# When a pair of weight blocks is asked for, and what stands in line behind its mixing: first pass of a decoder layer on one core

## The chip, the core and the metric

The kernel runs on one core of one Trainium2 chip. The metric is the device time of one execution in microseconds (us). The engines are TensorE (PE, with PEld for its weight loads), VectorE (DVE), ScalarE (ACT) and GpSimd (POOL); each works through its own queue strictly in order. SyncE (SP) issues all DMA transfers here, also in order: an entry that waits holds up every entry behind it.

## The reference

One layer over a sequence of 1024 positions and 2048 channels: x is projected by `w_in`, eight attention heads with a forget gate, a short convolution and a pooling branch work on the projections, each branch is gated, and everything is projected back and normalised:

```python
proj = einsum('bsd,de->bse', x, w_in)
q, k, v, g_att, fg, c_b, c_c, c_h, g_conv, p_u, g_pool = split(proj)
y = concat([attention(q, k, v, fg) * silu(g_att),
            short_conv(c_b, c_c, c_h) * silu(g_conv),
            pool(p_u) * silu(g_pool)])
out = layer_norm(alpha * x + einsum('bse,ed->bsd', y, w_out))
```

All is float32. A matmul operand is split into a rounded part and a remainder, and three matmuls stand for one.

## The kernel before, in words

Both projections are computed by a Strassen-Winograd scheme: the operands are cut in 2 x 2 blocks and seven block products take the place of eight. The weight columns of the input projection come as 28 pairs (`Pair`, N_PAIRS); a pair has four raw blocks of 128 x 1024 (512 KB each), numbered 0 to 3. From them are mixed T1 = block 1 - block 0, T2 = block 3 - T1, T3 = block 3 - block 1 and T4 = block 2 - T2 (`mix`, `mix_last`; T1 and T2 on DVE, T3 and T4 on POOL). T4 is stored to memory (`store_mixed`, t_dram) for the second pass.

The first pass (`first_pass`, up to the end of the pool "first") computes four products of every pair: "11" with block 0, "s2" with T2, "s1" with T1 and "s3" with T3. A product is 8 x 3 matmuls of 512 columns (`multiply`). For the pairs 0 to 11 (AHEAD) the product "11" is done at the start. The pairs are then worked in the order 0, 12, 1, 13, ..., 11, 23, 24 to 27; the index in this order is the place n. So an even place up to 22 has three products (s2, s1, s3) and an odd place four (11, s2, s1, s3).

While a product runs, the operand of the next one is split: ACT casts the rounded part (L121, "hi"), DVE subtracts it (L122, "lo"); both need two of four buffers h1, which come free when the product before has ended. The third matmul of a product is the first that needs lo. `beside(p, name)` says what else is issued after each product: the mixing of the pair at place n+1, the loading of the pair at place n+2 (`load_place`), the eight blocks s4 of x (`make_s4`, four loads of 256 KB from xt, three subtractions on DVE, one store to s4_dram), and the mixing of the output weights (`OutBlocks`: four loads from w_out, four subtractions on POOL, four stores to o_dram).

The order on each queue is set by a scheduler that runs when the program is built: it takes an instruction as soon as its model of the engines finds its inputs and a buffer ready, so it may pull an instruction in front of others that stand before it in the code. `tc.keep_in_program_order` pins an instruction to its place in the code. Raw blocks and T3 share nine buffers w1; s4 and the output weights use four buffers wr and some of wh. A load into a buffer waits for the last reader of what was in it. Each transfer also waits until the eighth before it has landed, since there are eight completion semaphores.

Of the kernel before, what the change touches and what calls it, by code (L numbers as in the profile page):

```python
# [36 lines left out]
ALU = mybir.AluOpType  # L37
# [4 lines left out]
S = 1024  # L42
# [3 lines left out]
H = S // 2  # L46
# [5 lines left out]
KH = KT // 2  # L52
N_PAIRS = 28
WARM_UP = 8
EARLY = 8
AHEAD = 12
# [17 lines left out]
def layer(ctx: ExitStack, tc: tile.TileContext, xt, x, wp, wf, b_f, conv_w, pool_w, pool_scale,  # L74
          w_out, ln_g, ln_b, out):
    nc = tc.nc
# [27 lines left out]
    def f4(name, tag):  # L104
        return tile_of([P, S], F32, name, tag)
# [50 lines left out]
    t_dram = dr.tile([N_PAIRS, P, S], F32, tag="td", name="t_dram")  # L156
    s4_dram = dr.tile([KH, P, H], F32, tag="s4d", name="s4_dram")
    sy_dram = dr.tile([4, KH, P, H], F32, tag="syd", name="sy_dram")
    o_dram = dr.tile([2, 4, KH, P, H], F32, tag="od", name="o_dram")
# [81 lines left out]
    class Pair:  # L241
# [12 lines left out]

        def mix(self):
            r = self.raw
            self.t3 = f4("t3", "w1")
            nc.gpsimd.tensor_tensor(self.t3, r[3], r[1], ALU.subtract)  # L258
            nc.vector.tensor_tensor(r[1], r[1], r[0], ALU.subtract)  # L259
            nc.vector.tensor_tensor(r[3], r[3], r[1], ALU.subtract)  # L260

        def mix_last(self):
            r = self.raw
            nc.gpsimd.tensor_tensor(r[2], r[2], r[3], ALU.subtract)  # L264

        def store_mixed(self):
            nc.sync.dma_start(t_dram[self.p], self.raw[2])

        def early(self, acc):

# [4 lines left out]
        def products(self):  # L275

            def start():
                self.ca = f4("ca", "c")
                if self.p < AHEAD:
                    nc.sync.dma_start(self.ca[:, :H], a_dram[self.p, :, :H])  # L280

            def p6():
                if self.ca is None:
                    start()
                self.b = bank("aux")
                return self.b

            def after_p6():
                self.u2 = half("u2", "wh")
                nc.vector.tensor_tensor(self.u2, self.b, self.ca[:, :H], ALU.add)  # L290

            def p5():
                self.c = bank("acc")
                return self.c

            def after_p5():
                self.cb = f4("cb", "c")
                nc.vector.tensor_tensor(self.cb[:, :H], self.c, self.u2, ALU.add)

            def after_p7():  # L300
                nc.vector.tensor_tensor(self.ca[:, H:], self.b, self.ca[:, :H], ALU.add)
                nc.vector.tensor_tensor(self.cb[:, H:], self.c, self.ca[:, H:], ALU.add)
                nc.sync.dma_start(a_dram[self.p], self.ca)
                nc.sync.dma_start(b_dram[self.p], self.cb)

            yield self, lambda: self.raw[3], "s2", p6, after_p6
            yield self, lambda: self.raw[1], "s1", p5, after_p5
            yield self, lambda: self.t3, "s3", lambda: self.b, after_p7

        def first_product(self):  # L310
# [46 lines left out]
            nc.tensor.transpose(turned[:, st], flat[:, st * P : st * P + P], ident[: 2 * NH, : 2 * NH])  # L357
        return turned

    def make_s4(k):  # L360
        r21, r22, r11, r12 = (half("xr", "wr") for _ in range(4))
        for r, e, h in ((r21, k, 1), (r22, KH + k, 1), (r11, k, 0), (r12, KH + k, 0)):
            nc.sync.dma_start(r, xt[e, :, h * H : h * H + H])
        nc.vector.tensor_tensor(r21, r21, r22, ALU.add)
        nc.vector.tensor_tensor(r21, r21, r11, ALU.subtract)
        nc.vector.tensor_tensor(r12, r12, r21, ALU.subtract)
        nc.sync.dma_start(s4_dram[k], r12)

    class OutBlocks:
# [5 lines left out]
        def load(self):  # L375
            i, k = self.i, self.k
            self.t = [half("wo", tag) for tag in ("wr", "wr", "wr", "wh")]
            for t, e, c in zip(self.t, (KH + k, KH + k, k, k), (0, 1, 0, 1)):
                nc.sync.dma_start(t, w_out[e, :, i * S + c * H : i * S + c * H + H])

        def mix(self):
            b11, b12, b21, b22 = self.t
# [6 lines left out]

        def store(self):  # L390
            for j, t in enumerate(self.t):
                nc.sync.dma_start(o_dram[self.i, j, self.k], t)

    pairs = [Pair(p) for p in range(N_PAIRS)]
    banks = [bank("acc") for _ in range(4)] + [bank("aux") for _ in range(4)]
# [54 lines left out]
    def load_place(n):  # L450
        order[n].load(0, 1, 3, 2)

    def beside(p, name):
# [10 lines left out]
        n = place[p]  # L464
# [3 lines left out]
        if name == "s2" and n < N_PAIRS - 2:  # L468
            pairs[p].store_mixed()
            if n - 1 in outs:  # L470
                outs[n - 1].store()
            if n in outs:
                outs[n].load()
        if name == "s1":
            if n in outs:
                outs[n].mix()
            if n in gate_sums_at:
                env["sums"] = gate_sums(gate_sums_at[n], 0)
        if name == "s3":
            if n + 2 < N_PAIRS:  # L480
                load_place(n + 2)
            if 3 <= n < 7:
                make_s4(2 * n - 6)
                make_s4(2 * n - 5)
            if n == 2:
                nc.vector.tensor_copy(fgt[:, :4], turned_sums(env["sums"]))
            if n == 3:
                nc.vector.tensor_tensor(fgt[:, 4:], fgt[:, :4], turned_sums(env["sums"]), ALU.subtract)
# [6 lines left out]
        if (n, name) == (N_PAIRS - 1, "s1"):  # L495
            replace("s4", "xc", s4_dram)
            for q in (0, 1):
                t = half("c11", "wr")
# [8 lines left out]

    banks_set = deque()
    env, gate_sums_at = {}, {2: "11", 3: "s3"}
    outs = {7 + n: OutBlocks(n % 2, n // 2) for n in range(2 * KH)}  # L510

    def first_pass():
        ahead_of = in_order()
# [739 lines left out]
```

## Time and profile before

| | us |
|---|---|
| median of 3 runs | 1677.95 (1676.4 to 1681.62) |
| profiled execution | 1684.7 |
| span of its trace | 1682.9 |

The start (products "11" of the first pairs) takes the first 85 us, the rest of the first pass lasts to about 692 us; then come the second pass with the attention, and the output projection. The output weights are mixed at the places 7 to 22, which lie between about 230 us and 575 us. PE is the busiest engine (1572.4 us); TensorE's granted clock is 0.973 of full speed on average. In the tables a wait is put down to what ended last, "x" is a count of instructions, and a time in a window counts from the start of the span.

### The profile page before, as it was taken

How to read it: one execution, taken by the hardware profiler on the slowest of the kernel's cores; microseconds unless marked ns; L12 is line 12 of the kernel's file. 1: busy time of each engine (PE TensorE's matmuls, PEld its weight loads, DVE VectorE, ACT ScalarE, POOL GpSimd, SP SyncE). 2: the span in 40 equal slices, each digit the busy share in tenths (PEclk: the TensorE clock that was granted, in tenths of full speed). 3: DMA queues.
4: the chain of work that ended last, by engine and by line, in shares of the span. 5: the costliest groups of instructions: out<-in, count | busy, mean ns of one | idle time of the engine just before them, and what ended most of it. 6: DMA issues, size and time to landing. Idle time of an engine off the chain costs nothing. (4 is left out here: it accounts for less than half of the span.)

```text
span 1682.9 us, 20233 instructions
## 1 busy us (share of the span) xinstructions
PE 1572.4 (93%) x6836; PEld 1268.7 (75%) x6836; DVE 1101.1 (65%) x1587; ACT 701.6 (42%) x1254; POOL 511.1 (30%) x381
## 2 busy tenths in 40 slices
PE   7999999899889899999999999989988899999985
PEld 6777887777767788788878787867766777788765
DVE  6786445445555445468777777776779875567777
ACT  4412221111111124457575757656665554434431
POOL 0133245555556521002222222342426221100005
PEclk9999999999999999999999999999999999999998
DMA  8986567778777754735454545445445446557562
GB/s 240 337 294 231 203 213 271 269 269 280 259 268 252 266 210 153 272 111 183 155 182 158 174 168 165 154 137 183 141 143 168 149 140 216 185 179 232 181 190 100
DMA packets 156808, 339.93 MB, mean 202 GB/s; under 512 B 17952, under 2 KB 27040, under 8 KB 156704
## 3 DMA queue, kind: packets, MB, share of 16 engines
q1 hardware_dynamic: 156704, 338.64, 59.7%
q8 instruction: 53, 0.87, 0.2%
q14 instruction: 51, 0.42, 0.1%
HBM read 247.28 MB, written 91.29 MB: 201 GB/s over the span
## 5 line engine op out<-in xcount | busy, mean ns | idle before, releaser
L122 DVE TENSOR_TENSOR wh<-wr,wh 128x512 fp32r<-128x512 f32 x272 | 204.8, 759 | 93.7 <-ACT wh L121 93.3
L121 ACT CAST wop<-wb 128x1024 fp32r<-128x1024 f32 x76 | 79.9, 1052 | 329.0 <-PE acc L129 199.7
L121 ACT CAST wh<-wr 128x512 fp32r<-128x512 f32 x272 | 166.5, 618 | 92.9 <-PE acc L130 34.4
L130 PE MATMUL aux<-xs,wop 128*128 128x512 f32 x448 | 178.7, 399 | 18.4 <-DVE wop L122 18.4
L128 PE MATMUL acc<-x,wh 128*128 128x512 f32 x448 | 178.7, 399 | 3.9 <-ACT wh L121 3.9
L130 PE MATMUL acc<-x,wh 128*128 128x512 f32 x448 | 177.7, 397 | 1.9 <-DVE wh L122 1.9
L128 PE MATMUL aux<-xs,wop 128*128 128x512 f32 x448 | 177.3, 396 | 0.0
L129 PE MATMUL aux<-xs,wop 128*128 128x512 f32 x448 | 177.2, 395 | 0.0
L129 PE MATMUL acc<-x,wh 128*128 128x512 f32 x448 | 176.1, 393 | 0.0
L122 DVE TENSOR_TENSOR wop<-wb,wop 128x1024 fp32r<-128x1024 f32 x76 | 126.1, 1659 | 55.0 <-ACT wop L121 55.0
L258 POOL TENSOR_TENSOR t<-wb,wb 128x1024 f32<-128x1024 f32 x28 | 69.7, 2490 | 304.0 <-DMA wb<-wp 131.2
L130 PEld LDWEIGHTS aux<-xs,wop 128*128 128x128 f32 x448 | 86.0, 192 | 39.7 <-DVE wop L122 21.6
L259 DVE TENSOR_TENSOR wb<-wb,wb 128x1024 f32<-128x1024 f32 x28 | 37.5, 1340 | 119.3 <-POOL t L258 119.3
L130 PEld LDWEIGHTS acc<-x,wh 128*128 128x128 f32 x448 | 84.6, 189 | 27.1 <-DVE wh L122 9.2
L128 PEld LDWEIGHTS acc<-x,wh 128*128 128x128 f32 x448 | 84.8, 189 | 23.7 <-ACT wh L121 8.2
L128 PEld LDWEIGHTS aux<-xs,wop 128*128 128x128 f32 x448 | 86.1, 192 | 18.1
L129 PEld LDWEIGHTS aux<-xs,wop 128*128 128x128 f32 x448 | 85.7, 191 | 18.3
L129 PEld LDWEIGHTS acc<-x,wh 128*128 128x128 f32 x448 | 84.9, 190 | 15.6
L264 POOL TENSOR_TENSOR wb<-wb,wb 128x1024 f32<-128x1024 f32 x28 | 81.7, 2919 | 38.9 <-DVE wb L260 36.0
L130 PE MATMUL acc<-xs,wh 128*128 128x512 f32 x224 | 88.1, 393 | 3.0 <-DVE wh L122 2.9
L688 POOL TENSOR_TENSOR m<-m,t 128x256 f32<-128x256 f32 (+1 forms) x64 | 69.9, 1092 | 62.7 <-ACT t L741 59.0
L121 ACT CAST wop<-t 128x1024 fp32r<-128x1024 f32 x28 | 29.5, 1054 | 141.3 <-PE aux L129 83.2
(265 smaller groups left out, 3859.8 us busy)
## 6 DMA issues: line engine op xcount, KB each, us to landing
wb<-wp SPq DMA_DIRECT2D x116, 512.0 KB, 5.7
wr<-wp SPq DMA_DIRECT2D x112, 256.0 KB, 2.9
wo<-w_out SPq DMA_DIRECT2D x64, 256.0 KB, 5.2
o_dram<-wo SPq DMA_DIRECT2D x64, 256.0 KB, 3.0
wr<-o_dram SPq DMA_DIRECT2D x64, 256.0 KB, 2.8
t_dram<-wb SPq DMA_DIRECT2D x28, 512.0 KB, 3.8
a_dram<-ca SPq DMA_DIRECT2D x28, 512.0 KB, 6.0
b_dram<-cb SPq DMA_DIRECT2D x28, 512.0 KB, 6.1
```

Source lines behind the costliest of these rows:

```text
L121: nc.scalar.copy(hi, src)
L122: nc.vector.tensor_tensor(lo, src, hi.bitcast(F32), ALU.subtract)
L128: nc.tensor.matmul(acc, wh, xh, start=start, stop=False, **more)
L129: nc.tensor.matmul(acc, wh, xl, start=False, stop=False, **more)
L130: nc.tensor.matmul(acc, wl, xh, start=False, stop=stop, **more)
L258: nc.gpsimd.tensor_tensor(self.t3, r[3], r[1], ALU.subtract)
L259: nc.vector.tensor_tensor(r[1], r[1], r[0], ALU.subtract)
L264: nc.gpsimd.tensor_tensor(r[2], r[2], r[3], ALU.subtract)
L688: eng.tensor_tensor(kept[n][:, c0:], prev[:, c0:], t[n, j][:, c0:], op)
```

## The change

Four things change in the first pass. (1) `load_place(n + 2)` is issued after product s1 of place n, where it was after s3. (2) For the pairs 0 to 11, whose block 0 is no longer needed, T1 is written over block 0, T2 into a new buffer and T3 over block 1; the instructions stand in the order T1, T2, T3. For the other pairs all stays as it was: T3 into a new buffer first, then T1 over block 1 and T2 over block 3. (3) The loads and stores of the output weights, the store of T4 and the loads of s4 are pinned to their place in the code; the s4 blocks are loaded after one product and mixed after the next of s2 and s3, from place 3 to place 7. (4) The output weights are mixed at the places 7 to 24 without 14 and 18.

```diff
         def mix(self):
             r = self.raw
-            self.t3 = f4("t3", "w1")
-            nc.gpsimd.tensor_tensor(self.t3, r[3], r[1], ALU.subtract)
-            nc.vector.tensor_tensor(r[1], r[1], r[0], ALU.subtract)
-            nc.vector.tensor_tensor(r[3], r[3], r[1], ALU.subtract)
+            if self.p < AHEAD:
+                self.t1, self.t2, self.t3 = r[0], f4("t2", "w1"), r[1]
+                nc.vector.tensor_tensor(self.t1, r[1], r[0], ALU.subtract)
+                nc.vector.tensor_tensor(self.t2, r[3], self.t1, ALU.subtract)
+                nc.gpsimd.tensor_tensor(self.t3, r[3], r[1], ALU.subtract)
+            else:
+                self.t1, self.t2, self.t3 = r[1], r[3], f4("t3", "w1")
+                nc.gpsimd.tensor_tensor(self.t3, r[3], r[1], ALU.subtract)
+                nc.vector.tensor_tensor(self.t1, r[1], r[0], ALU.subtract)
+                nc.vector.tensor_tensor(self.t2, r[3], self.t1, ALU.subtract)
...
         def store_mixed(self):
-            nc.sync.dma_start(t_dram[self.p], self.raw[2])
+            tc.keep_in_program_order(nc.sync.dma_start(t_dram[self.p], self.raw[2]))
...
-    def make_s4(k):
+    s4_parts = {}
+
+    def load_s4(k):
         r21, r22, r11, r12 = (half("xr", "wr") for _ in range(4))
         for r, e, h in ((r21, k, 1), (r22, KH + k, 1), (r11, k, 0), (r12, KH + k, 0)):
-            nc.sync.dma_start(r, xt[e, :, h * H : h * H + H])
+            tc.keep_in_program_order(nc.sync.dma_start(r, xt[e, :, h * H : h * H + H]))
+        s4_parts[k] = r21, r22, r11, r12
+
+    def make_s4(k):
+        r21, r22, r11, r12 = s4_parts.pop(k)
...
             for t, e, c in zip(self.t, (KH + k, KH + k, k, k), (0, 1, 0, 1)):
-                nc.sync.dma_start(t, w_out[e, :, i * S + c * H : i * S + c * H + H])
+                src = w_out[e, :, i * S + c * H : i * S + c * H + H]
+                tc.keep_in_program_order(nc.sync.dma_start(t, src))
...
             for j, t in enumerate(self.t):
-                nc.sync.dma_start(o_dram[self.i, j, self.k], t)
+                tc.keep_in_program_order(nc.sync.dma_start(o_dram[self.i, j, self.k], t))
...
+        if name in ("s2", "s3") and 3 <= n < 8:
+            for k in s4_parts.copy():
+                make_s4(k)
+            if n < 7:
+                load_s4(2 * n - 6 + (name == "s3"))
         if name == "s1":
             if n in outs:
                 outs[n].mix()
+            if n + 2 < N_PAIRS:
+                load_place(n + 2)
...
         if name == "s3":
-            if n + 2 < N_PAIRS:
-                load_place(n + 2)
-            if 3 <= n < 7:
-                make_s4(2 * n - 6)
-                make_s4(2 * n - 5)
...
-    outs = {7 + n: OutBlocks(n % 2, n // 2) for n in range(2 * KH)}
+    out_places = [n for n in range(7, 25) if n not in (14, 18)]
+    outs = {n: OutBlocks(m % 2, m // 2) for m, n in enumerate(out_places)}
```

Three places show what this does to the queues. The first is SP's queue in the start, about where the last weights of the early products (we) and the last rows of x (xrow) are asked for; xr are the s4 loads. Before:

```order
L234 DMA xrow_458<-xt 128x512
L363 DMA xr_1272<-xt 128x512
L363 DMA xr_1273<-xt 128x512
L363 DMA xr_1274<-xt 128x512
L222 DMA we_473<-wp 128x8x128
L218 DMA xrow_375<-xt 128x512
```

and now:

```order
L234 DMA xrow_458<-xt 128x512
L222 DMA we_473<-wp 128x8x128
L218 DMA xrow_375<-xt 128x512
L233 DMA xrow_508<-xt 128x512
L234 DMA xrow_508<-xt 128x512
```

All 32 s4 loads have left the start; the first four now stand behind the T4 store of place 3.

The second place is DVE's queue about the mixing of the pair at place 14 (an even place). wop_2539 (before) and wop_2547 (now) are lo of the same product, "11" of place 13; u, cb and ca are the sums after s2, s1 and s3 of place 12. Before:

```order
L259 TENSOR_TENSOR wb_2572<-wb_2572,wb_2570 128x1024
L298 TENSOR_TENSOR cb_2531<-acc_2506,u_400_2482 128x512
L260 TENSOR_TENSOR wb_2574<-wb_2574,wb_2572 128x1024
L122 TENSOR_TENSOR wop_2539<-wb_2443,wop_2538 128x1024
L301 TENSOR_TENSOR ca_2455<-aux_2457,ca_2455 128x512
```

and now:

```order
L259 TENSOR_TENSOR wb_2538<-wb_2540,wb_2538 128x1024
L296 TENSOR_TENSOR u_400_2482<-aux_2457,ca_2455 128x512
L122 TENSOR_TENSOR wop_2503<-wb_2257,wop_2502 128x1024
L304 TENSOR_TENSOR cb_2531<-acc_2506,u_400_2482 128x512
L122 TENSOR_TENSOR wop_2547<-wb_2411,wop_2546 128x1024
L260 TENSOR_TENSOR t_421_2609<-wb_2542,wb_2538 128x1024
L307 TENSOR_TENSOR ca_2455<-aux_2457,ca_2455 128x512
```

T1 (L259) now stands one product earlier, ahead of u, and T2 (L260) behind the lo that it stood ahead of. At the odd places, T1 moved from ahead of cb to behind it, and T2 behind the lo of the next s2.

The third place is DVE's queue at the places 3 and 4, where the s4 subtractions (L376 to L378) now stand; wop_1249, wop_1299 and wop_1350 are lo of the products s2, s1 and s3 of place 4:

```order
L122 TENSOR_TENSOR wop_1249<-t_181_1145,wop_1248 128x1024
L266 TENSOR_TENSOR wb_1225<-wb_1225,wb_1223 128x1024
L378 TENSOR_TENSOR xr_1287<-xr_1287,xr_1284 128x512
L259 TENSOR_TENSOR wb_1380<-wb_1382,wb_1380 128x1024
L307 TENSOR_TENSOR ca_1143<-aux_1154,ca_1143 128x512
L503 TENSOR_TENSOR fgt<-fgt,aux_1292 128x64
L122 TENSOR_TENSOR wop_1299<-wb_1049,wop_1298 128x1024
L308 TENSOR_TENSOR cb_1219<-acc_1194,ca_1143 128x512
L376 TENSOR_TENSOR xr_1341<-xr_1341,xr_1342 128x512
L377 TENSOR_TENSOR xr_1341<-xr_1341,xr_1343 128x512
L378 TENSOR_TENSOR xr_1344<-xr_1344,xr_1341 128x512
L296 TENSOR_TENSOR u_211_1329<-aux_1304,ca_1302 128x512
```

Before, no s4 instruction stood here. Now three of them stand ahead of nearly every lo from place 3 to place 8, and the fourth load of an s4 block goes into the buffer from which the block before is stored.

## Rows read from the trace of the kernel before

**Rows 1.** The profile's page: PE's busy time, and GB/s moved in 40 slices.
```profile
PE 1572.4 (93%) x6836; PEld 1268.7 (75%) x6836; DVE 1101.1 (65%) x1587; ACT 701.6 (42%) x1254; POOL 511.1 (30%) x381
...
GB/s 240 337 294 231 203 213 271 269 269 280 259 268 252 266 210 153 272 111 183 155 182 158 174 168 165 154 137 183 141 143 168 149 140 216 185 179 232 181 190 100
```

**Rows 2.** Stretches: length, busy (count) by engine, clock, DMA share, GB/s.
```profile
148.90:289.50 140.60, 140.60 (x623) 114.55 (x622) 70.45 (x69) 28.45 (x31) 52.09 (x24) 1.00 0.65 227
289.50:645.90 356.40, 325.55 (x1370) 264.01 (x1369) 178.70 (x155) 64.22 (x67) 184.55 (x88) 0.96 0.72 250
```

**Rows 3.** ACT's casts on the timeline: start, length, instruction, idle time before.
```profile
186.05 1.05 ACT L121 CAST wop<-wb 128x1024 fp32r<-128x1024 f32 x1 [4.34 <-PE acc L129]
...
213.25 1.05 ACT L121 CAST wop<-wb 128x1024 fp32r<-128x1024 f32 x1 [4.39 <-PE aux L129]
```

**Rows 4.** PE's waits between 250 and 660 us: total, times, longest.
```profile
PE acc L130 <- DVE wop L122: 16.0, 8, 4.9
PE aux L130 <- DVE wop L122: 14.9, 6, 4.6
```

**Rows 5.** DVE on the timeline from 430 us.
```profile
430.37 1.92 DVE L122 TENSOR_TENSOR wop<-t,wop 128x1024 fp32r<-128x1024 f32 x1 [0.15 <-ACT wop L121]
440.48 1.23 DVE L259 TENSOR_TENSOR wb<-wb,wb 128x1024 f32<-128x1024 f32 x1 [8.19 <-POOL t L258]
...
443.35 1.22 DVE L122 TENSOR_TENSOR wop<-wb,wop 128x1024 fp32r<-128x1024 f32 x1
```

**Rows 6.** POOL, SP and PE in the same stretch.
```profile
438.05 2.40 POOL L258 TENSOR_TENSOR t<-wb,wb 128x1024 f32<-128x1024 f32 x1 [6.84 <-DMA wb<-wp]
...
431.24 0.32 SPq L392 DMA_DIRECT2D o_dram<-wo  x1
431.61 0.50 SPq L252 DMA_DIRECT2D wb<-wp  x1
...
444.63 0.50 PE L130 MATMUL acc<-x,wop 128*128 128x512 f32 x1 [3.86 <-DVE wop L122]
```

**Rows 7.** Two stretches behind a stall, columns as in rows 2.
```profile
336.00:339.40 3.40, 3.28 (x8) 2.62 (x9) 3.35 (x4) 0.00 (x0) 3.40 (x2) 0.50 0.73 250
339.40:354.00 14.60, 14.60 (x66) 11.97 (x64) 5.17 (x6) 2.45 (x3) 4.82 (x3) 1.00 0.97 310
```

**Rows 8.** From issue to landing of all loads of raw blocks.
```profile
DMA to landing us min/median/max: 2.6/5.4/9.3
```

**Rows 9.** POOL's groups, 250 to 600 us: count, busy, mean ns, idle before.
```profile
L264 POOL TENSOR_TENSOR wb<-wb,wb 128x1024 f32<-128x1024 f32 x15 | 41.7, 2780 | 0.0
...
L385 POOL TENSOR_TENSOR wo<-wo,wo 128x512 f32<-128x512 f32 x16 | 32.5, 2032 | 1.2
```

**Rows 10.** The start on the timeline: SP, ACT and PE.
```profile
32.20 3.23 SPq L363 DMA_DIRECT2D xr<-xt  x3
...
43.48 0.62 ACT L121 CAST x<-xrow 128x512 fp32r<-128x512 f32 x1 [6.67 <-DMA xrow<-xt]
...
44.16 2.07 PE L128 MATMUL acc<-x,weh 128*128 128x512 f32 x4 [5.54 <-ACT x L121]
```

**Rows 11.** DVE, POOL and PE about 85 us.
```profile
81.66 2.91 DVE L364 TENSOR_TENSOR xr<-xr,xr 128x512 f32<-128x512 f32 x1
84.49 3.39 DVE L259 TENSOR_TENSOR wb<-wb,wb 128x1024 f32<-128x1024 f32 x1
...
83.97 2.83 POOL L264 TENSOR_TENSOR wb<-wb,wb 128x1024 f32<-128x1024 f32 x1
...
89.07 0.50 PE L130 MATMUL aux<-xs,wop 128*128 128x512 f32 x1 [3.54 <-DVE wop L122]
```

**Rows 12.** Landing of s4 loads (32) and s4 stores (8), from their two lines.
```profile
DMA to landing us min/median/max: 2.6/6.1/8.0
...
DMA to landing us min/median/max: 3.7/5.4/6.2
```

**Rows 13.** Transfers between 250 and 600 us: count, KB each, median us to landing.
```profile
o_dram<-wo SPq DMA_DIRECT2D x63, 256.0 KB, 3.0
wo<-w_out SPq DMA_DIRECT2D x59, 256.0 KB, 5.1
```

More of the change, by code (lines that the diff above doesn't have):

```diff
@@ L256, in mix @@
             r = self.raw
-            self.t3 = f4("t3", "w1")
-            nc.gpsimd.tensor_tensor(self.t3, r[3], r[1], ALU.subtract)
-            nc.vector.tensor_tensor(r[1], r[1], r[0], ALU.subtract)
-            nc.vector.tensor_tensor(r[3], r[3], r[1], ALU.subtract)
+            if self.p < AHEAD:
[8 more added lines that the diff above has]
+                nc.vector.tensor_tensor(self.t2, r[3], self.t1, ALU.subtract)
         def mix_last(self):
             r = self.raw
-            nc.gpsimd.tensor_tensor(r[2], r[2], r[3], ALU.subtract)
+            nc.gpsimd.tensor_tensor(r[2], r[2], self.t2, ALU.subtract)
         def store_mixed(self):
-            nc.sync.dma_start(t_dram[self.p], self.raw[2])
+            tc.keep_in_program_order(nc.sync.dma_start(t_dram[self.p], self.raw[2]))
         def early(self, acc):
@@ L304, in after_p7 @@
                 nc.sync.dma_start(b_dram[self.p], self.cb)
-            yield self, lambda: self.raw[3], "s2", p6, after_p6
-            yield self, lambda: self.raw[1], "s1", p5, after_p5
+            yield self, lambda: self.t2, "s2", p6, after_p6
+            yield self, lambda: self.t1, "s1", p5, after_p5
             yield self, lambda: self.t3, "s3", lambda: self.b, after_p7
```

## The prediction

> **What bounds the kernel now.** I read the page first: PE is busy 1572.4 us of the span, nothing else comes near [rows 1], so time is lost only where PE waits or runs slowly. Then the first pass cut in stretches. From 148.9 to 289.5 us PE is busy throughout and the granted clock is 1.00; from 289.5 to 645.9 us it is busy 325.55 of 356.4 us at a mean clock of 0.96 [rows 2]. The order of products says that the second stretch is the places 10 to 25: seven even places with 3 products, seven odd ones with 4 and two more with 4, that is 57. A product takes 5.44 us when nothing waits: ACT's casts, one per product, stand at 186.05 and, five later, at 213.25 [rows 3]. 57 x 5.44 is 310.1 us, so 46.3 us are lost here.
>
> The waits say to what: 14 waits of PE, 30.9 us together, all for lo of the running product, none over 4.9 us [rows 4]. One of them, read backwards: PE resumes at 444.63 after 3.86 us; lo was split at 443.35. It could have been split about 436, but DVE stood 8.19 us before T1 (L259), which waits for T3 on POOL, since T1 overwrites the block that T3 reads; T3 stood 6.84 us until the raw block landed. That block had been asked for at 431.61, right behind a store of output weights [rows 5, 6]. So a late load holds T3, T3 holds T1, and T1 holds a lo that has nothing to do with it. The other 15.4 us of the loss are the slower clock behind a stall: after a wait of 3.87 us TensorE is granted 0.50, the lower of its levels (1.2 GHz), and does 8 matmuls in 3.4 us, where 66 in 14.6 us (15.4 in 3.4) go at full clock [rows 7]. That is 7.4 matmuls, or 1.7 us per dip.
>
> **The change part by part.** The sum is made against the profiled execution (1684.7 us); the median of the runs is 6.75 us lower (0.4%), and I subtract the same difference from it.
>
> *The start.* Three s4 loads no longer stand before the last-but-two rows of x on SP. They are 0.79 MB; PE waits 5.54 us for those rows [rows 10]. At the best slice of the page, 337 GB/s [rows 1], 0.79 MB take 2.3 us; SP spent 3.23 us issuing them [rows 10]. Bounds 0 (the rows would be late anyway) and 3.2; I take 2.3, because the transfers run back to back here. Next late is nothing else: this product then starts 2.3 us sooner and so does all behind it. At 85 us PE waits 3.54 us for a lo behind an s4 subtraction of 2.91 us and a T1 of 3.39 us [rows 11]. The s4 instruction goes, and T1 of the first pair is written over block 0 and stands far ahead. I take the whole wait and the dip behind it: 3.54 + 1.7 = 5.2 us; bounds 0 and 5.2.
>
> *Loads one product sooner, and T1 without T3.* No wait is over 4.9 us and a product is 5.44 us: if the loads really come one product sooner, all 14 waits go, with 46.3 us. At the even places T1 also loses the 2.40 us of T3 [rows 6]. At the odd places T1 still stands behind T3, so there I work out what is late next. In the new queues the last load that T3 of an odd place needs stands behind the output-weight stores, and these behind POOL: T4 of the pair before (2.78) and three subtractions of 2.03 at most [rows 9] make 8.9 us after T2 of that pair, which is done about 0.5 us before product "11" begins. Add landing 5.4 (2.6 to 9.3) [rows 8], T3 2.40 [rows 6], T1 1.23 and lo 1.22 [rows 5]: 19.1 us. Lo is due with the third matmul of the fourth product after, 0.5 + 4 x 5.44 + 2 x 0.227 = 22.7 us. So 3.6 us are spare at the median landing, and 0.3 us are missing at the longest. The lower bound of the gain: the waits ahead of s2 of the even places, which come from odd pairs, all stay (14.9 of 30.9 us, with their part of the dips 22.3 us), so 24.0 us are gained. The upper bound is 46.3. I take 38, nearer the upper, since only the longest landings are late.
>
> *Neighbouring engine.* T3 of an even pair now runs on POOL beside DVE's splits instead of before them. Row: T1 takes 1.23 us alone [rows 5] and 3.39 us beside T4 on POOL [rows 11]. The Trainium skill, "GPSIMD Engine Reference", section "Specifications", says that POOL shares its SBUF interfaces with VectorE and contends with instructions that have two SBUF inputs; the trace agrees (1.23 against 3.39), and by that rule alone the 12 early pairs would each lose about 2.2 us on DVE. A lo has 5.44 - 1.05 - 1.22 = 3.2 us to spare [rows 3, 5], so 2.2 us are hidden and I charge nothing; together with another delay they are not.
>
> *s4 in the places 3 to 8.* Here the cover was complete (clock 1.00, no wait [rows 2]), and here the change adds work. Each of eight rounds is: four loads, three subtractions, one store; the fourth load goes into the buffer that the store before it empties. So a round cannot be shorter than store, load and one subtraction (0.69 us, as long as a DVE operation of half a 1.23 us one). With their landings [rows 12]: at the shortest 3.7 + 2.6 + 0.7 = 7.0 us, at the medians 5.4 + 6.1 + 0.7 = 12.2 us. From the other transfers of 256 KB between 250 and 600 us, 3.0 + 5.1 + 0.7 = 8.8 us [rows 13]. In DVE's queue the last subtraction of round 0 stands ahead of lo of s3 at place 3, that of round 7 ahead of lo of s2 at place 7: twelve products, 65.3 us, for seven rounds, 9.3 us each. Queued behind each waiting subtraction are u, T1 or T2, and a lo; PE waits for the lo. At 7.0 or 8.8 us a round nothing is lost; at 12.2 us, 20 us and seven dips of 1.7, 32 us. The load on the transfers there rises from 227 GB/s by 8 x 1.31 MB in 140.6 us, 75 GB/s, to 302, between the 250 of [rows 2] and the start's 337. I take a round of 10.3 us, half way between 8.8 and 12.2: 7 us, and one dip, 9 us.
>
> *The rest.* Output weights at the places 23 and 24 fall where the loss is one short wait; I charge nothing. The places 14 and 18 without them only ease SP. Behind the first pass the queues are as before.
>
> Sum: 2.3 + 5.2 + 38 - 9 = 36.5 us; 1684.7 becomes 1648, and the median 1677.95 becomes 1641.
>
> **The rivals.** (a) *The odd pairs keep their waits.* For it: their T1 still waits for T3, and 14.9 us come from them [rows 4]. Against: 3.6 us spare. Gain 24 instead of 38: 1655. (b) *The loads do not come sooner*: the scheduler already issued them as soon as a buffer was free, whatever their place in the code, so only T3's 2.40 us go from the eight waits ahead of "11", the sum 16.0; taken from each, at most 12 us, with dips 18. 1677.95 - 18 - 7.5 + 9 is 1661. Against: in SP's new order the four loads of place n+2 stand before the T4 store of n+1. (c) *The s4 rounds decide: slower.* Place: the buffers of the fourth loads, places 3 to 8. For it: the round of 12.2 us at the medians of these very transfers. With the gains of the start and the 38, a loss of 45.5 us is needed to end level: (round - 9.3) x 7 + 12 of dips, so a round of 14.1 us; at 15 us the price is 52 us and the time 1684. Against: even the longest landings, 6.2 + 8.0 + 0.7, make 14.9, and all would have to be so long.
> The Trainium skill, "DMA: Bandwidth & Descriptors", section "Specifications", gives about 358 GB/s as the memory's limit for a core; the page's slices stay below (337 at most). Around the s4 rounds alone, some 76 us, its rule would speak for (c).
>
> **How the numbers follow.** The forecast has 0.60, (a) 0.18, (b) 0.12, (c) and its like 0.10, part of which ends near level. What a measurement of this kernel can tell from no change is about 0.3%, 5 us. Faster by more: 0.88; within: 0.05; slower by more: 0.07. The lower end takes all gains and no price of s4: 2.3 + 1.7 (a shorter dip at 44 us) + 5.2 + 46.3 = 55.5, 1622. The upper end lies past (b) with its s4 price at 16 us: 1668. The forecast's own range is 1625 to 1655.
>
> **What would show it.** Right: no wait of PE at 38 to 44 us longer than about 3.3 us and none at 85 us; in the places 10 to 25 fewer than six waits for lo, and DVE's idle time before T1 down from 8 us to below 3; some waits of PE for lo behind L376 to L378 at the places 3 to 8, 5 to 12 us in all with dips. Wrong: PE waits for lo at each even place still (a); T3 still waiting about 7 us for raw blocks (b); waits of 2 us or more at six or more products between 150 and 250 us (c), or waits in the second pass that were not there.

## The result

The changed kernel takes 1661.04 us (median of 4 runs, 1659.66 to 1662.88); the kernel before took 1679.74 us beside it (4 runs). The ratio is 0.989, 95% interval 0.987 to 0.991: faster, by 18.7 us. The forecast was 1641 us, a gain twice as large; the result lies outside the forecast's own range (1625 to 1655). The profiled executions lie further apart: 1684.7 us before, 1661.48 us now, 23.2 us. One execution of the kernel of experiment 9 was disturbed, took 4153 us and counts in no number below.

The page after, first row, answers to the first of [rows 1]:

```profile
PE 1561.2 (94%) x6836; PEld 1258.9 (76%) x6836; DVE 1116.7 (67%) x1587; ACT 701.0 (42%) x1254; POOL 517.4 (31%) x381
```

To see where the time went, I counted PE's matmuls of the first pass in groups of 24 and so found where each product begins. Four boundaries are enough: the first product s2 (place 0) begins at 82.3 us (before 84.9), place 3 at 140.8 (148.9), place 10 at 289.8 (289.4), place 26 at 626.8 (645.9). The trace of the changed kernel cut there, columns as in [rows 2]:

```profile
82.30:140.80 58.50, 58.50 (x262) 46.65 (x260) 28.13 (x28) 12.46 (x14) 19.64 (x7) 1.00 0.51 179
140.80:289.80 149.00, 143.01 (x623) 113.81 (x622) 89.39 (x91) 28.40 (x31) 46.55 (x21) 1.00 0.81 285
289.80:626.80 337.00, 319.50 (x1369) 260.24 (x1368) 198.25 (x155) 64.30 (x66) 191.59 (x88) 0.98 0.76 266
```

The places 3 to 9 hold 25 products, 136.0 us at 5.44 each; they took 140.5 us before and take 149.0 now. The places 10 to 25 hold 57, 310.1 us; they took 356.5 and take 337.0. Below, the "loss" of a stretch is its length less 136.1 or 310.2 us, a tenth more, since the boundaries are read to a tenth:

| us | begin of place 3 | loss, places 3 to 9 | loss, places 10 to 25 |
|---|---|---|---|
| before | 148.9 | 4.5 | 46.3 |
| changed | 140.8 | 12.9 | 26.9 |

The 4.5 us before in the places 3 to 9 are no lost time: PE was busy throughout at full clock, and 20 matmuls of the forget gate's sums stand between the products there, 0.227 us each. They stand there in every kernel below, so only what a kernel has above 4.5 is lost.

So 8.1 us were gained in the start, 8.4 lost in the places 3 to 9, 19.4 gained behind. That is 19.1 us at place 26. Another 4.4 us of the 23.5 us between the spans came in the later passes, which the change doesn't touch: from place 26 to the end it is 1037.0 us before and 1032.6 now, and in the kernels below anything from 1032.3 to 1039.7. PE's waits in the places 10 to 25, answering to [rows 4]:

```profile
PE aux L130 <- DVE wop L122: 15.4, 8, 3.6
PE acc L130 <- DVE wop L122: 2.1, 2, 1.1
```

The eight waits ahead of "11" (16.0 us) have gone; the 2.1 us now on acc are ahead of s1, at the places 10 and 12. On aux the sum stays (14.9 to 15.4), but not the places: before, all six waits stood ahead of s2 of an even place; now five do (10.8 us), and three (4.6 us) are new, ahead of s2 of the places 23, 24 and 25. One of the five, at place 18, on DVE, POOL and PE of the changed kernel; it answers to [rows 5, 6]:

```profile
425.98 1.23 DVE L260 TENSOR_TENSOR t<-wb,wb 128x1024 f32<-128x1024 f32 x1 [1.67 <-DMA wb<-wp]
...
449.54 1.23 DVE L265 TENSOR_TENSOR wb<-wb,wb 128x1024 f32<-128x1024 f32 x1 [4.86 <-POOL t L264]
450.68 2.28 DVE L122 TENSOR_TENSOR wop<-t,wop 128x1024 fp32r<-128x1024 f32 x1
```

```profile
426.05 3.43 POOL L261 TENSOR_TENSOR wb<-wb,wb 128x1024 f32<-128x1024 f32 x1 [10.14 <-DMA wo<-w_out]
429.44 2.27 POOL L397 TENSOR_TENSOR wo<-wo,wo 128x512 f32<-128x512 f32 x1
431.67 2.39 POOL L270 TENSOR_TENSOR wb<-wb,t 128x1024 f32<-128x1024 f32 x1
434.02 2.33 POOL L398 TENSOR_TENSOR wo<-wo,wo 128x512 f32<-128x512 f32 x1
436.43 1.28 POOL L399 TENSOR_TENSOR wo<-wo,wo 128x512 f32<-128x512 f32 x1
437.79 1.29 POOL L400 TENSOR_TENSOR wo<-wo,wo 128x512 f32<-128x512 f32 x1
447.11 2.40 POOL L264 TENSOR_TENSOR t<-wb,wb 128x1024 f32<-128x1024 f32 x1 [8.03 <-DMA wb<-wp]
```

```profile
453.02 0.80 PE L130 MATMUL aux<-xs,wop 128*128 128x512 f32 x1 [3.17 <-DVE wop L122]
```

And SP's queue between them (DMA issues only):

```profile
430.83 1.18 SPq L273 DMA_DIRECT2D t_dram<-wb  x1
436.38 0.32 SPq L405 DMA_DIRECT2D o_dram<-wo  x1
436.75 0.42 SPq L252 DMA_DIRECT2D wb<-wp  x1
437.74 1.69 SPq L405 DMA_DIRECT2D o_dram<-wo  x3
439.48 1.15 SPq L392 DMA_DIRECT2D wo<-w_out  x2
440.67 0.46 SPq L252 DMA_DIRECT2D wb<-wp  x1
```

Read backwards: PE waits for a lo (L122, 450.68). It stands behind T1 of the next odd pair (L265), which waits for T3 (POOL L264), which waits for a raw block. That block was asked for at 440.67, behind three stores of output weights and two loads. SP could issue the stores only as POOL's subtractions L398 to L400 ended, and these stand behind T3, L397 and T4 (L261 and L270 are T3 and T4 of the even pair).

### The profile page after: what moved, and what is told of

The parts are those of the page before. It is cut to its first block, busy times and chain, and to the rows that moved or that the text cites. A ratio compares the mean times of both kernels' runs of the same rounds, so it can differ in the third digit from the quotient of the medians.

```text
span 1659.4 us, 20213 instructions
## 1 busy us (share of the span) xinstructions
PE 1561.2 (94%) x6836; PEld 1258.9 (76%) x6836; DVE 1116.7 (67%) x1587; ACT 701.0 (42%) x1254; POOL 517.4 (31%) x381
## 3 DMA queue, kind: packets, MB, share of 16 engines
q1 hardware_dynamic: 156704, 338.64, 60.2%
## 5 line engine op out<-in xcount | busy, mean ns | idle before, releaser
L122 DVE TENSOR_TENSOR wh<-wr,wh 128x512 fp32r<-128x512 f32 x272 | 203.2, 753 | 94.7 <-ACT wh L121 94.1
L130 PE MATMUL aux<-xs,wop 128*128 128x512 f32 x448 | 178.4, 398 | 18.7 <-DVE wop L122 18.6
L122 DVE TENSOR_TENSOR wop<-wb,wop 128x1024 fp32r<-128x1024 f32 x76 | 120.6, 1587 | 41.6 <-ACT wop L121 41.5
L130 PE MATMUL acc<-xs,wh 128*128 128x512 f32 x224 | 87.8, 392 | 3.4 <-DVE wh L122 3.4
L130 PE MATMUL acc<-xs,wop 128*128 128x512 f32 x224 | 87.7, 392 | 2.3 <-DVE wop L122 2.1
L704 POOL TENSOR_TENSOR m<-m,t 128x256 f32<-128x256 f32 (+1 forms) x64 | 69.9, 1092 | 63.2 <-ACT t L757 61.0
L128 PE MATMUL acc<-xs,wh 128*128 128x512 f32 x224 | 88.2, 394 | 0.0
L122 DVE TENSOR_TENSOR pt<-t,pt 128x512 fp32r<-128x512 f32 (+1 forms) x96 | 84.0, 888 | 6.3 <-ACT pt L121 6.1
L129 PE MATMUL acc<-xs,wh 128*128 128x512 f32 x224 | 87.4, 390 | 0.0
```

The lines of the kernel that those rows point to most:

```text
L122: nc.vector.tensor_tensor(lo, src, hi.bitcast(F32), ALU.subtract)
L128: nc.tensor.matmul(acc, wh, xh, start=start, stop=False, **more)
L129: nc.tensor.matmul(acc, wh, xl, start=False, stop=False, **more)
L130: nc.tensor.matmul(acc, wl, xh, start=False, stop=stop, **more)
L704: eng.tensor_tensor(kept[n][:, c0:], prev[:, c0:], t[n, j][:, c0:], op)
```

## The experiments

The theory after the result: what holds up the places 10 to 25 is the order on SP, raw blocks behind stores that wait for POOL. Rivals: T1's place behind T3 costs by itself; the nine buffers w1 bind; the transfers take too long. Losses are read from each run's trace as above. A ratio is to the kernel before, with its 95% interval.

**1. The early load alone.** The kernel before with

```diff
         if name == "s1":
...
+            if n + 2 < N_PAIRS:
+                load_place(n + 2)
...
         if name == "s3":
-            if n + 2 < N_PAIRS:
-                load_place(n + 2)
```

> The kernel before with one edit alone: load_place(n+2) after s1 instead of s3. Theory (late raw blocks hold T3, T3 holds T1): the blocks land up to 5.4 us sooner, so the waits of PE at the places 10 to 25 (30.9 us before) fall to about half, and the time by 8 to 20 us; the waits at 38 and 85 us stay, since the s4 loads still stand in the start. Rival (the scheduler already asks for a block when a buffer is free, so the place in the code does nothing): within 3 us of before, waits as before.

Measured: 1.0007 (0.9991 to 1.0022), loss of the places 10 to 25 43.6 us. The rival held in its number: moving the loads in the code brought 2.7 us in these places and nothing in the time. SP waited as long for POOL as in the kernel before (in each, the first of four lines for the output weights' stores; the lines are of the kernel before, then of this one):

```profile
SPq L392 <- POOL wo L384: 60.2, 13, 8.2
```

```profile
SPq L392 <- POOL wo L384: 64.5, 14, 7.6
```

**2. The order T1, T2, T3 alone.** The kernel before with the new `mix` for the pairs 0 to 11:

```diff
+            if self.p < AHEAD:
+                self.t1, self.t2, self.t3 = r[0], f4("t2", "w1"), r[1]
+                nc.vector.tensor_tensor(self.t1, r[1], r[0], ALU.subtract)
...
```

> The kernel before with one edit alone: T1 over block 0, T2 into a new buffer, T3 last, for the pairs 0 to 11. Theory (in the changed kernel the eight waits ahead of product 11 fell from 16.0 to 2.1 us because T1 no longer stands behind T3): those waits fall to about 4 us here too and the six ahead of s2 of the even places (14.9 us) stay; with the half-clock stretches that is 15 to 20 us less. Rival (the earlier load did it): at most 2.4 us from each wait, some 5 us less in all.

Measured: 0.9864 (0.9842 to 0.9887), no less than the whole change. The loss of the places 10 to 25 is 24.1 us. The waits ahead of "11" fell as expected, from 16.0 to 3.3. Those ahead of s2 of the even places, expected to stay, went too; new ones, more but shorter, stand in s3 (the first two lines):

```profile
PE aux L130 <- DVE wop L122: 9.3, 9, 1.5
PE aux L128 <- DVE u L296: 3.9, 5, 1.4
PE acc L130 <- DVE wop L122: 3.3, 2, 2.7
```

So of the four parts this one brings as much as all four together; what the other three win and lose leaves nothing that the ratios can tell.

**3. s4 spread.** The changed kernel with one s4 block per place:

```diff
-        if name in ("s2", "s3") and 3 <= n < 8:
+        if name == "s2" and 1 <= n < 10:
...
-            if n < 7:
-                load_s4(2 * n - 6 + (name == "s3"))
+            if n < 9:
+                load_s4(n - 1)
...
-    out_places = [n for n in range(7, 25) if n not in (14, 18)]
+    out_places = range(9, 25)
```

> The changed kernel with one s4 block per place at the places 1 to 8 (loaded after s2 of one place, mixed after s2 of the next, where it was two blocks per place at 3 to 7) and the output weights at the places 9 to 24. Theory (the rounds of load, subtraction, store cost 10.3 us between 166 and 302 us, because seven of them are packed in twelve products): a round now has 3 to 4 products, 16 to 22 us; the waits between 200 and 292 us go and the time falls by 8 to 10 us, to about 1652. Rival (it is the amount of transfers in these places, not the chain): waits of the same sum move to the places 1 to 8, time within 3 us of 1661.

Measured: 0.988 (0.9856 to 0.9905), no better. The places 5 to 9 were free of waits as expected, but the loss of 3 to 9 stayed at 12.3 us: one product took 10.7 us. Its lo stands behind T1, and T1 waited 4.28 us for a raw block, which SP asked for only at 170.45 us, behind the store of an s4 block at 169.10:

```profile
176.35 1.23 DVE L259 TENSOR_TENSOR wb<-wb,wb 128x1024 f32<-128x1024 f32 x1 [4.28 <-DMA wb<-wp]
177.49 0.68 DVE L308 TENSOR_TENSOR cb<-acc,ca 128x512 f32<-128x512 f32 x1
178.09 1.22 DVE L122 TENSOR_TENSOR wop<-wb,wop 128x1024 fp32r<-128x1024 f32 x1
```

The theory falls, and the rival's numbers came out: waits of much the same sum (5.2 us of PE, 5.7 in the changed kernel), now at the places 2 to 4, and a time within 3 us. The run doesn't say whether the transfers or the store in the queue make that block late.

**4. The odd pairs mixed like the even ones.** The changed kernel with

```diff
-            if self.p < AHEAD:
...
-        if name == ("s2" if p < AHEAD else "11") and n + 1 < N_PAIRS:
-            order[n + 1].mix()
...
+        after = order[n + 1] if n + 1 < N_PAIRS else None
+        if after and name == ("s3" if after.p >= AHEAD and n < N_PAIRS - 2 else "11"):
+            after.mix()
...
```

> The changed kernel with the odd pairs mixed like the even ones: T1 over block 0 once product 11's operand is split, T2 into a new buffer, T3 last; their mixing stands one product later in the code. Theory (the eight waits ahead of s2 of the even places, 15.4 us, are there because T1 of the next odd pair stands in DVE's queue and waits for T3, and T3 for a raw block): those waits go, with their half-clock stretches 12 to 20 us, to about 1643. Rival (the raw block is late whoever reads it): T1 and T2 wait for the same blocks, only T3's 2.40 us go from each of the waits, 5 to 8 us less.

Measured: 0.9968 (0.9949 to 0.9988), the changed kernel stands at 0.989, so this is some 13 us slower; loss of the places 10 to 25 26.4 us and of 3 to 9 18.7. The theory as I had it (T3 is what holds T1) falls: without T3 ahead of it, T1 waits for the block itself, and PE's waits move to s2 of the odd places and s1 of the even ones. The block is late whoever reads it:

```profile
DVE wb L258 <- DMA wb<-wp: 13.6, 4, 4.5
```

**5. Output weights behind the raw blocks.** The changed kernel with

```diff
-            if n - 1 in outs:
-                outs[n - 1].store()
-            if n in outs:
-                outs[n].load()
...
         if name == "s1":
-            if n in outs:
-                outs[n].mix()
             if n + 2 < N_PAIRS:
                 load_place(n + 2)
+            if n < N_PAIRS - 2:
+                if n - 1 in outs:
+                    outs[n - 1].store()
+                if n in outs:
+                    outs[n].load()
...
         if name == "s3":
+            if n in outs:
+                outs[n].mix()
```

> The changed kernel with the store and the loads of output weights issued after s1, behind the raw blocks of place n+2, and mixed after s3 (they stood after s2, ahead of them). Theory (what keeps a raw block late in the places 10 to 25 is its place in SP's queue, behind stores of output weights that wait for POOL's subtractions): the blocks are asked for about 5 us sooner, the delays of those places, 26.9 us in the changed kernel, fall below 15, and the time by 10 us or more. Rival (a block waits for one of the nine buffers w1, which its reader, a lo of place n, frees): SP waits as long at L252, now with the output weights queued behind; delays 20 to 30 us, time within 4 us of the changed kernel or later.

The subtractions of the output weights move with them, from behind s1 to behind s3.

Measured: 0.9742 (0.9715 to 0.9769), 1640.04 us. The loss of the places 10 to 25 is 9.6 us; the row answers to the last of [rows 2]:

```profile
282.70:602.50 319.80, 314.19 (x1370) 257.20 (x1368) 168.90 (x152) 64.41 (x67) 167.48 (x88) 0.99 0.83 279
```

SP still waits at L252, where the raw blocks are asked for, and for long: for the buffers that a lo or the T4 store frees (60.8 and 89.0 us there). But this hurts little.

**6. Without POOL's subtractions of the output weights** (one execution). `OutBlocks.mix` keeps the four blocks as they were loaded, so this kernel leaves out part of the layer's computation:

```diff
-            t3 = half("wo", "wh")
-            nc.gpsimd.tensor_tensor(t3, b22, b12, ALU.subtract)
-            nc.gpsimd.tensor_tensor(b12, b12, b11, ALU.subtract)
-            nc.gpsimd.tensor_tensor(b22, b22, b12, ALU.subtract)
-            nc.gpsimd.tensor_tensor(b21, b21, b22, ALU.subtract)
-            self.t = b12, b22, t3, b21
+            self.t = b12, b22, b11, b21
```

> The changed kernel without the four subtractions of the output weights on POOL (their blocks are stored as they were loaded, so that part of the computation is left out). Theory (SP waits for these subtractions with raw blocks behind it, and T3 stands behind them on POOL): the delays of the places 10 to 25 fall from 26.9 to below 12 us. Rival (buffers w1 or the transfers' own time): above 20 us. The lo's of 2.3 us beside POOL become rarer by either.

Measured: 1633.68 us, loss of the places 10 to 25 0.3 us, with as many transfers as before and the clock at full speed:

```profile
282.30:592.80 310.50, 310.50 (x1370) 256.56 (x1369) 154.87 (x152) 64.48 (x67) 81.75 (x32) 1.00 0.80 284
```

The transfers' own time and the nine buffers are out as causes: both are as they were. But it takes the waits from SP's stores and, at once, the work from POOL; experiments 5 and 11 keep the work.

**7. A buffer more.** The changed kernel with

```diff
-FIRST = {"w1": (4, 9), "c": (4, 4), ...
+FIRST = {"w1": (4, 10), "c": (4, 3), ...
```

> The changed kernel with ten buffers w1 where it had nine (and three buffers c for the sums, where it had four, to make room). Theory (queue of SP behind POOL): a buffer more changes little, delays of the places 10 to 25 within 4 us of 26.9, unless the sums' fewer buffers add some. Rival (buffers): SP's waits at L252 for a lo or for T2, 89 us in all between 290 and 650 us, fall to less than half, and the delays to below 15 us.

Measured: 0.9997 (0.9978 to 1.0017), loss 34.4 us. SP waits longer for POOL (first line 52.3 us in 10; 30.3 in 9 in the changed kernel) and no less for buffers. The rival does not hold, but the run doesn't say what the tenth buffer alone would do, since the sums lost one.

**8. s4 as before.** The changed kernel with the old `make_s4`, not pinned.

```diff
-    def load_s4(k):
...
         if name == "s3":
+            if 3 <= n < 7:
+                make_s4(2 * n - 6)
+                make_s4(2 * n - 5)
```

> The changed kernel with s4 loaded and mixed as before the change (not pinned, so that its first loads return to the start); all else as changed. Theory (the s4 rounds cost 8.5 us in the places 3 to 9 and give back about 1.3 us at 38 us): the delays of the places 3 to 9, 8.5 us over the kernel before, go, the wait at 38 us returns to 5.5 us, and the time falls by 5 to 8 us, to about 1655. Rival (the delays there come from the raw blocks asked for sooner, and the s4 loads only stand beside): they stay, and the time is 1661 or later.

Measured: 0.9862 (0.9839 to 0.9885). The loss of the places 3 to 9 is 4.5 us again, so the 8.4 us came with the new s4:

```profile
142.30:282.80 140.50, 140.50 (x621) 114.46 (x621) 73.77 (x68) 28.39 (x31) 50.98 (x22) 1.00 0.68 228
282.80:623.30 340.50, 318.95 (x1369) 259.20 (x1368) 202.07 (x154) 64.36 (x67) 187.29 (x88) 0.98 0.75 263
```

Behind them 3.4 us more were lost, and place 3 began 1.5 us later, so 3.5 us of the 8.4 are left at place 26. The time was expected to fall by 5 to 8 us; by the ratio (0.989 for the changed kernel, the intervals overlap) the runs can't tell whether anything is left at the end.

**9. The old mixing behind the new order.** Experiment 5 with the kernel before's `mix`:

```diff
-            if self.p < AHEAD:
-                self.t1, self.t2, self.t3 = r[0], f4("t2", "w1"), r[1]
...
```

> outs_behind with the mixing of all pairs as in the kernel before (T3 first, T1 behind it). Theory (the loss of the places 10 to 25 needs both: a T3 in front of T1, and a raw block that comes late since it stands behind the output weights in SP's queue; with the blocks in time T3 is early and T1 never waits for it): delays of the places 10 to 25 of 10 to 18 us, where the kernel before has 46.3, only_early 43.6 and outs_behind 9.6; time about 1645. Rival (T1 behind T3 costs by itself, whenever the block comes): above 25 us, time 1658 or more.

> The kernel of behind_oldmix once more, for a profile that can be set beside the others: with a time near 1638 the theory (the blocks in time, T3 never late) expects delays of the places 10 to 25 of 6 to 14 us and no idle time of DVE over 4 us before T1 that POOL's T3 ended; the rival (the gain came from elsewhere) expects delays above 20 us there and a shorter start or second pass.

Measured: 0.9734 (0.969 to 0.9778), from three executions of 1632.01 to 1641.06 us; the execution whose trace is read here took 1631.22 us. The loss of the places 10 to 25 is none:

```profile
285.30:595.40 310.10, 310.10 (x1370) 256.86 (x1369) 161.19 (x152) 64.45 (x67) 169.49 (x88) 1.00 0.86 288
```

T1 behind T3 costs nothing by itself. With the blocks in time the new mixing even costs in this stretch: experiment 5 loses 9.6 us, and there T1 of the even pairs waits 29.4 us in 6 waits for its block, ahead of a lo. In the places 3 to 9 it is the other way (7.5 us in 5, 12.1 here), and the ratios are level.

**10. Experiment 5 with s4 as before, and with s4 spread** (the edits of 8 and 3).

> outs_behind with s4 loaded and mixed as before the change. Theory (s4 in the places 3 to 8 costs there what s4_as_before gave back, 8.4 us of 12.9; in outs_behind only 7.4 us are lost there, of which 4.5 stay, and about 1.5 us come back at 38 us): 1 to 2 us faster than outs_behind, near 1638. Rival (unpinned s4 loads now fall among the raw blocks and hold them up): slower than outs_behind by 3 us or more.

> outs_behind with one s4 block per place at the places 1 to 8 and the output weights at the places 9 to 24. Theory (the one long wait of s4_spread, at 176 us, was T1 in front of a lo with its raw block late behind s4 loads that wait for a store): that wait stays, some 5 us, the rest of the places 3 to 9 is free, and 10 to 25 as in outs_behind: within 4 us of outs_behind. Rival (with the output weights moved two places later, POOL is late at the end): 1645 or more.

Measured: 0.9762 (0.9723 to 0.98) and 0.9858 (0.9825 to 0.9891). The first is level with experiment 5: 2.9 us less lost in the places 3 to 9, but place 3 begins 4.7 us later. The second is slower: losses of 12.8 in the places 3 to 9, as in experiment 3, and 16.4 behind. Both expectations were too good. Of the second one's rival the time came true (1645 or more; 1657.21 us), but its loss lies at the places 14 to 22, not at the end; its cause is open.

**11. The order on SP, without the rest of the change.** The kernel before with the raw blocks behind s1 and the output weights, pinned, behind them; T4's store pinned; the mixing of the pairs, s4 and the places of the output weights untouched (the edit of 5, with three times `tc.keep_in_program_order`). As in 5, the subtractions of the output weights move on POOL, from behind s1 to behind s3.

> The kernel before with the raw blocks asked for after s1 and, behind them, the pinned stores and loads of output weights, which are mixed after s3; T4's store pinned; mixing order, s4 and the places of the output weights as before. Theory (the order on SP is the whole of it): delays of the places 10 to 25 below 15 us where before has 46.3, those of 3 to 9 stay at 4.5, the waits at 38 and 85 us (5.5 and 3.5) stay, about 1645. Rival (it also takes the places 7 to 24 or the mixing of the even pairs): above 25 us, 1658 or more.

Measured: 0.9725 (0.9686 to 0.9764), 1636.47 us, the lowest ratio of all these kernels, though level within the intervals with experiments 5 and 9. The stretches 3 to 9 and 10 to 25:

```profile
146.80:287.30 140.50, 140.50 (x622) 114.48 (x622) 70.00 (x69) 28.42 (x31) 50.83 (x22) 1.00 0.69 225
287.30:597.60 310.30, 310.30 (x1369) 256.64 (x1368) 157.11 (x152) 64.38 (x67) 168.80 (x88) 1.00 0.87 291
```

The loss of 10 to 25 went from 46.3 to 0.1 us. T1's idle time behind T3 there, before and in this kernel (total, times, longest):

```profile
DVE wb L259 <- POOL t L258: 93.3, 16, 8.2
```

```profile
DVE wb L259 <- POOL t L258: 27.6, 9, 4.9
```

T1 still waits for T3, but no longer so long that a lo is late. (Another 20.2 us of its idle time, in 7 waits, end by the profile with the landing of a store, and no lo is late behind them either.) T3 itself waited for the raw blocks before, and no longer does (lines of the kernel before, then of this one):

```profile
POOL t L258 <- DMA wb<-wp: 106.2, 14, 9.4
```

```profile
POOL t L258 <- DMA wb<-wp: 8.9, 2, 6.2
```

In these 14 waits before, POOL stood idle until a block landed. So its subtractions held up T3 through what SP had to wait for, not as work ahead of T3 on POOL. But no run moves the subtractions alone: part of the gain can come from T4's store, at which SP waited 20.8 us in 15 waits for POOL before and not at all now. And SP's waits for POOL at the stores, 101.3 us in the kernel before (60.2, 24.1, 13.8 and 3.2 by subtraction), are 8.7 us:

```profile
SPq L392 <- POOL wo L387: 5.8, 11, 1.2
...
SPq L392 <- POOL wo L386: 2.9, 7, 1.2
```

SP now waits at the raw blocks instead, as in 5 (61.4 us for a lo, 63.2 us for T4's store to land).

**12. The fourth s4 load in a buffer of its own.** Experiment 9 with

```diff
-        r21, r22, r11, r12 = (half("xr", "wr") for _ in range(4))
+        r21, r22, r11, r12 = (half("xr", tag) for tag in ("wr", "wr", "wr", "wh"))
```

> The kernel of behind_oldmix with the fourth block of an s4 round (r12) in a buffer of wh, where it shared the four of wr. Theory (a round's last load waits for the landing of the store before it, so the last subtraction and the lo's behind it are late): the delays of the places 3 to 9, 12.1 us in old_mix_again, fall to 4.5 to 8 and the time to 1626 to 1632. Rival (the store of s4 itself holds up SP's queue, 29.3 us in eight waits for the last subtraction, whatever buffer the load has; or the rounds' amount of transfers): delays of 10 us or more there, time as behind_oldmix.

Measured: 0.9782 (0.9747 to 0.9817), loss of the places 3 to 9 18.1 us where the same kernel without the edit lost 12.1. The theory falls: SP's waits at an s4 load for the landing of the store before (6.7 us in 6 without the edit) are gone, and the loss has grown. The fourth load's buffer is not what makes a round long. The rival's numbers hold (10 us or more), but it names two causes.

## Why the prediction was wrong, and what of it was right

*The places 10 to 25* are the step that failed: 38 us were forecast there, 19.4 were measured. The prediction held that "if the loads really come one product sooner, all 14 waits go", and that for the odd places the last load comes "8.9 us after T2", so "3.6 us are spare". At place 18, T2 ended at 427.2 us and the load was issued at 441.1: 13.9 us later instead of 8.9. The sum had only T4 and three subtractions on POOL behind T2. It left out T3 of the even pair, which the change itself put there (3.43 us, of which 2.3 fell behind T2's end), and the first subtraction (2.27): T4 starts 4.5 us after T2's end. T4 and the three subtractions then took 7.4 us, 1.5 less than forecast; but after the last of them SP spent another 2.0 us on a store, two loads and the raw load itself, which the sum left out as well. The lo took 2.28 us beside POOL's work, not 1.22. With the landing (6.0 from there to T3's start) that is 13.9 + 6.0 + 2.4 + 1.2 + 2.3 = 25.8 us against the 22.7 allowed: 3.1 us late; 3.17 measured.

Behind the sum stands a wrong reading. [rows 6] show the raw block at 431.61 right behind a store at 431.24, and I read it as a late load, where it is late stores with a load behind them: by the trace SP had waited 9.8 us for POOL at the four stores of output weights ahead of it, 6.1 of them at the first. (The buffer it writes came free at 431.56, when another pair's T4 store, which had waited for POOL too, landed; so there both held it.) Moving the load in the code changes nothing while the store stays in front (experiment 1); taking the store's wait away (6) or the store from in front of the blocks (11) gives all of it.

Two rivals came true in part. (a), the odd pairs keep their waits, set 24.0 us: five of the waits ahead of s2 of the even places are there. (b), the loads do not come sooner, set 1661, the measured time, and its sign is there too: T3 still waits for raw blocks, 42.6 us in 5 waits at the odd pairs and 24.6 in 4 at the even ones, longest 12.2. But its reason was a buffer's coming free, where the load at 440.67 waited for nothing but the entries ahead of it; and it let the waits ahead of "11" fall by 12 us of 16.0, where all went. That its time fits so closely is luck.

The output weights at the places 23 and 24, at which I charged nothing, were not free either: 7.1 us of the 26.9 are lost at s2 of the places 23 to 25 (before, 5.0 ahead of "11" of 23 and 24). At place 25, with a wait of 3.30 us, it is another chain than at place 18. T3 stands on POOL right behind the first subtraction, which waited for a load of output weights; by the trace the raw block had landed 3.2 us before T3's start:

```profile
600.99 1.28 POOL L397 TENSOR_TENSOR wo<-wo,wo 128x512 f32<-128x512 f32 x1 [12.82 <-DMA wo<-w_out]
602.23 2.40 POOL L264 TENSOR_TENSOR t<-wb,wb 128x1024 f32<-128x1024 f32 x1
```

*The start* came out right in its sum, 7.5 us forecast and 8.1 measured, and in one of its two terms. The wait at 85 us is gone [rows 11]: between 82.3 and 140.8 us PE is busy throughout, in the first row of stretches above, and 5.4 us shorter than before, where 5.2 were forecast. Either part of the change does that: of the wait 0.3 us are left with the new mixing alone (2), 0.6 with the old s4 (8), 0.4 with the old mixing (9), and 3.5 and 4.0 where neither is there (1 and 11). The other 2.7 us lie ahead of place 0, and the term of 2.3 for the s4 loads is not shown. The wait at 38 us fell from 5.54 [rows 10] only to 4.25 us, where the prediction's sign was 3.3; and experiment 11, with the s4 loads as before and a wait of 5.5 us there, reaches place 0 at 82.1 us, no later than the changed kernel.

```profile
40.96 0.79 PE L128 MATMUL acc<-x,weh 128*128 128x512 f32 x1 [4.25 <-ACT x L121]
```

*The s4 rounds* came out right in size, by luck, and wrong in their reason. 9 us were forecast, 8.4 measured and given back by experiment 8. (The round of 10.3 us is not half way between 8.8 and 12.2, as the prediction says; that is 10.5.) From the first s4 store (152.9 us) to the eighth (228.6) a round takes 10.8 us. But it is not mainly the fourth load that is late. In the places 3 to 9 DVE waits at the first subtraction (and only 1.5 us at the last, which needs the fourth load), and SP at the store:

```profile
DVE xr L376 <- DMA xr<-xt: 19.1, 5, 4.6
```

```profile
SPq L379 <- DVE xr L378: 19.8, 7, 4.8
```

The store of a round stands in SP's queue ahead of the next round's loads, and waits there for the last subtraction. That looks like the pattern of the output weights; experiment 12 excludes the buffer, but no run tested the store's place. And half of the 8.4 us fall at the places 8 and 9, behind the last s4 store: there SP waits 10.2 us at a store of output weights for POOL (L398). Why the old s4 gives that half back too is open.

*What was right of T1 behind T3*: with late blocks, T1 ahead of T3 spares those waits (experiment 2, some 22 us of loss). It treats the symptom: with the blocks in time it is worth nothing or less in these places (9 and 5).

*The end of the first pass* was as forecast: from place 26 on the products take 46.8 us, as before.

## What to carry to other kernels

Where an operand is late, follow its load back to the queue that issues it, and look at the entry ahead of it: a store that waits for a slow engine holds up every load behind it. Here an earlier request brought nothing and reordered arithmetic about half of the loss; letting the two change places brought all of it. When a chain is summed to see whether a deadline holds, list everything that the change itself queues on each engine of the chain; here half of the 4.5 us that the sum left out on POOL were an instruction that the change had put there. A loss seen at several consumers in turn (T1, T3, lo) can have one source upstream: take that one away first, and measure what the downstream cures are still worth.

## What the runs showed that I had not expected

The transfers were not short of room in the kernel before. In the places 10 to 25 the DMA engines were busy 72% of the time before (250 GB/s) and 87% (291 GB/s) in experiment 11, where the trace shows no wait of PE for lo. The Trainium skill ("DMA: Bandwidth & Descriptors", section "Specifications") gives about 358 GB/s as a core's limit; none of these stretches comes near enough to show it. And POOL and DVE side by side cost no time as long as the blocks came early: POOL worked 184.7 us in that stretch before and 168.8 us in experiment 11, and the lo's slowed beside it (2.28 us instead of 1.22 in the stretch shown first, up to 2.21 in experiment 11) have room for that. The Trainium skill ("GPSIMD Engine Reference", section "Specifications") says that POOL contends with VectorE's instructions that have two SBUF inputs; the traces agree (1.22 against 2.28 us). In experiment 11 PE lost 0.1 us in these places to everything together, so it had no price there.
